# Output projection as 2x2 blocks with seven products for each two row tiles

## The chip, the core and the metric

The kernel runs on one core of one Trainium2 chip. The metric is the device time of one execution in microseconds (us). Five engines run their own instruction streams: TensorE (PE in the rows, with its weight loads as PEld), VectorE (DVE), ScalarE (ACT), GpSimd (POOL), and SyncE (SP), which here issues nearly all DMAs. They meet only through semaphores.

## The reference

One layer over 1024 tokens of width 1024, all in float32. Two branches (an attention `y_a` and a gated mixing branch `y_b`, each 512 wide) are projected up, gated and added; the sum goes through one output projection, is added to the input and normalised:

```python
p_a = jnp.einsum('bse,ed->bsd', y_a, w_up_a[l])
p_b = jnp.einsum('bse,ed->bsd', y_b, w_up_b[l])
merged = jax.nn.sigmoid(g_a) * p_a + jax.nn.sigmoid(g_b) * p_b
x = x + jnp.einsum('bsd,de->bse', merged, w_out[l])
...
return rmsnorm(x, final_norm_g)
```

## The kernel before

A float32 product is made of three matmuls on float32r operands: every operand is split into a high part (a cast on ACT, `copy`, L157) and a low part (the difference, `tt`, L167), and high x high, high x low and low x high are summed in PSUM. `hi_lo` (L214) issues the cast and the difference; the difference is on DVE unless the call names POOL.

The input projection already works by blocks: `project` (L528) takes two output tiles against two halves of the contraction and makes their four results by 7 products instead of 8, with the combinations of the small operand made on the fly (`s1` to `s4`) and those of the large one (`T`) once. Attention heads, projections and branch work are interleaved.

What this document looks at are the three last stages:

- `up_b` (L899) projects branch b up: 8 column tiles `e` by 2 halves of 512 tokens, 12 matmuls each; results go to DRAM (`merged_b`).
- `up_a` (L946) does the same for branch a, first half 0, then half 1. For each unit `up` (L882) loads the gate, runs 12 matmuls of 512 columns, multiplies PSUM by the gate on DVE; `merge` (L939) loads branch b's tile, adds it on DVE, and splits the sum into `m_hi` and `m_lo` (one cast, one more DVE operation). The 8 weights of `w_up_a` are split once (`wa`, L936) and serve both halves.
- The output projection: `out_unit` (L976) runs 24 matmuls of 512 columns (8 contraction tiles by 3) for one tile of 128 tokens and one half of the columns, with a slice of `m_hi` or `m_lo` as the stationary operand and `w_out`, split by `wo_parts` (L922), as the moving one. There are 16 such units; the last is cut into two of 256 columns. Behind each unit DVE adds `x`, ACT squares and sums; behind the second column half come the sum, the reciprocal root on POOL, and the two scaled halves go out.

The order of each engine is fixed when the program is built. `Plan.add` records every operation; `issue` (L234) plays them with a cost of its own for each and lets each engine take, of what is ready, the operation with the smallest number; a number can be moved ahead with `pl.offset` (`ahead`, L813, does this by 6000), except for PE. Every engine then runs its list strictly in that order, so that an operation that waits holds up all behind it. Buffers have tags with a fixed number of slots ("a" 7, "b" 8, "f2" 6, "T" 14, and the PSUM banks X, Y, Z, o once, z twice); a load is issued by SP, in SP's order, when a slot is free.

Of the kernel before, what the change touches and what calls it, by code (L numbers as in the profile page):

```python
# [329 lines left out]
def hybrid_block(  # L330
# [197 lines left out]
    def project(g, use, keep=True):  # L528

        use_at, pl.offset = pl.offset, -9000  # L530

# [5 lines left out]
        raw = {}  # L537
        for q in ((0, 0), (1, 0), (1, 1), (0, 1)):
            raw[q] = buf("a", (P, 4, P))
            pl.load(raw[q].all, w_pairs[g, 2 * q[0] + q[1]].rearrange("p (k e) -> p k e", e=P))  # L540
# [22 lines left out]
        pl.tt(s2.all, s1.all, raw[0, 0].all, ALU.subtract)  # L563
# [9 lines left out]
        pl.tt(s3.all, raw[0, 0].all, raw[1, 0].all, ALU.subtract, eng="POOL")  # L573
# [335 lines left out]
    m_hi, m_lo = [], []  # L909
    for e in range(8):  # L910
        if e < 6:
            mt = buf("T", (P, 2, S), F32R)
            m_hi.append(mt[:, 0, :])
            m_lo.append(mt[:, 1, :])
        else:
            m_hi.append(buf("k", (P, S), F32R).all)
            m_lo.append(buf("k", (P, S), F32R).all)

    wo = [[], []]
    wo_tags = ["r"] * 4 + ["e"] * 4 + ["ak"] * 2 + ["f1"] * 2  # L920

    def wo_parts(kt, c):  # L922
        raw = buf("a")
        pl.load(raw.all, w_out[kt, :, c * 512:c * 512 + 512])
        if c == 0:
            if kt < 6:
                hi, lo = [buf(tag, dt=F32R).all for tag in wo_tags[2 * kt:2 * kt + 2]]
            else:
                t = buf("k", (P, 2, 512), F32R)
                hi, lo = t[:, 0, :], t[:, 1, :]  # L930
        else:
            hi, lo = wo1[kt // 4][0][:, kt % 4, :], wo1[kt // 4][1][:, kt % 4, :]
        pl.hi_lo(hi, lo, raw.all)
        wo[c].append((hi, lo))
# [115 lines left out]
```

## Time and profile before

| | us |
|---|---|
| median of 3 runs | 766.98 (766.76 to 767.42) |
| the profiled execution | 766.53 |
| its span in the trace | 764.7 |
| PE busy in the span | 735.0 (96%) |
| DVE busy | 575.0 (75%) |
| ACT busy | 433.5 (57%) |
| POOL busy | 308.8 (40%) |

The span is what the trace shows; 1.8 us of the execution lie outside it. PE is busy nearly all the time, so the end of the kernel is set by how much PE has to do and by the places where it waits. A busy share says little about the other engines: what matters is whether PE waits for them at one place.

### The profile page before, as it was taken

What the parts mean: (1) busy time and instruction counts of PE and PEld (TensorE: products, weight loads), DVE (VectorE), ACT (ScalarE), POOL (GpSimd) and SP (SyncE); (2) the same over time, 40 slices, a digit from 0 to 9 for tenths busy, and PEclk for the clock granted to TensorE, in tenths of its full rate; (3) what the DMA queues carried; (4) which work ended last, traced back from release to release, by engine and by line L of the source; (5) the groups of instructions that cost most, each with busy time, mean ns of one, the idle gap of its engine ahead of it and who ended that gap; (6) DMA issues with size and microseconds to landing.
All of it is one profiled execution on the core that took longest, in us unless ns stands there. A gap on an engine that the chain in (4) does not pass through costs nothing.

```text
span 764.7 us, 10791 instructions
## 1 busy us (share of the span) xinstructions
PE 735.0 (96%) x3524; PEld 606.4 (79%) x3524; DVE 575.0 (75%) x788; ACT 433.5 (57%) x920; POOL 308.8 (40%) x298
## 2 busy tenths in 40 slices
PE   4989999999889999999999999999999999999996
PEld 3877788888777888887888888878888887888885
DVE  4868754688899787898999988897998878841122
ACT  6636474756756755666757676676867433411122
POOL 1500637497666576274345538234140300013110
PEclk9999999999999999999999999999999999999999
DMA  9412494424344375454543656354597677760022
GB/s 338 176 64 96 144 255 159 146 96 138 113 127 127 103 212 185 141 166 137 153 124 114 191 165 180 108 137 127 173 311 255 213 237 231 252 228 1 29 82 111
DMA packets 69177, 121.31 MB, mean 159 GB/s; under 512 B 7296, under 2 KB 17024, under 8 KB 69120
## 3 DMA queue, kind: packets, MB, share of 16 engines
q1 hardware_dynamic: 67968, 118.52, 49.3%
q10 hardware_dynamic: 1152, 2.10, 0.7%
q8 instruction: 28, 0.46, 0.3%
q14 instruction: 29, 0.24, 0.1%
HBM read 81.27 MB, written 39.32 MB: 158 GB/s over the span
## 4 chain that ended last, share of the span: by engine, by line
PE 83%; DVE 9%; issue 3%; DMA 2%; ACT 2%; POOL 1%; SPq 0%; POOLq 0%; DVEq 0%; ACTq 0%
PE Y L129 22%; PE X L129 21%; PE Z L129 18%; PE z L129 9%; PE o L129 8%; PE tr L133 5%; DVE b L167 2%; DVE ak L198 1%; DVE ak L191 1%; DMA k<-in_x_dram 1%; DVE e L167 1%; DMA k<-d 1%; DVE T L167 1%; DVE f L167 1%; DVE r L167 1%
## 5 line engine op out<-in xcount | busy, mean ns | idle before, releaser
L129 PE MATMUL Y<-T,b 128*128 128x512 f32 x672 | 180.0, 398 | 1.6 <-ACT b L157 1.3
L129 PE MATMUL X<-T,b 128*128 128x512 f32 x660 | 177.9, 398 | 0.0
L129 PE MATMUL Z<-T,b 128*128 128x512 f32 x540 | 145.2, 397 | 0.0
L129 PEld LDWEIGHTS Y<-T,b 128*128 128x128 f32 x672 | 122.3, 188 | 26.0 <-ACT b L157 1.7
L157 ACT CAST b<-a 128x512 fp32r<-128x512 f32 (+1 forms) x152 | 93.6, 617 | 81.9 <-PE Y L129 22.5
L129 PEld LDWEIGHTS X<-T,b 128*128 128x128 f32 x660 | 119.8, 188 | 22.8 <-POOL b L167 0.4
L167 DVE TENSOR_TENSOR b<-a,b 128x512 fp32r<-128x512 f32 (+1 forms) x112 | 99.4, 889 | 28.8 <-ACT b L157 20.0
L129 PEld LDWEIGHTS Z<-T,b 128*128 128x128 f32 x540 | 98.1, 188 | 18.3
L167 POOL TENSOR_TENSOR b<-a,b 128x512 fp32r<-128x512 f32 x40 | 60.7, 1516 | 119.8 <-ACT b L157 106.6
L198 DVE TENSOR_TENSOR_SCAN ak<-ak,c 128x128 f32<-128x128 f32 (+1 forms) x64 | 72.8, 1141 | 3.5 <-ACT ak L146 3.4
L167 POOL TENSOR_TENSOR a<-a,a 128x512 f32<-128x512 f32 x40 | 61.5, 1537 | 28.9 <-DVE b L167 15.3
L167 POOL TENSOR_TENSOR f<-f,f 128x512 f32<-128x512 f32 (+1 forms) x38 | 56.2, 1484 | 36.0 <-ACT f L146 14.7
L157 ACT CAST e<-tr 128x512 fp32r<-128x512 f32 (+1 forms) x96 | 45.7, 480 | 36.5 <-PE tr L133 33.3
L167 POOL TENSOR_TENSOR r<-r,ak 128x512 f32<-128x512 f32 x32 | 46.9, 1474 | 39.4 <-DVE ak L191 33.4
L133 PE MATMUL tr<-c,r 128*128 128x128 f32 x320 | 58.5, 273 | 2.6 <-DVE r L167 2.5
L129 PE MATMUL o<-e,k 128*128 128x512 f32 (+1 forms) x192 | 57.6, 343 | 3.3 <-DVE e L167 3.2
L146 ACT ACTIVATE ak<-z 128x128 f32<-128x128 f32 (+2 forms) x96 | 47.4, 494 | 20.4 <-PE z L129 18.1
L129 PE MATMUL z<-k,k 128*128 128x512 f32 (+2 forms) x216 | 56.8, 352 | 0.9 <-DMA k<-d 0.9
L167 DVE TENSOR_TENSOR e<-tr,e 128x512 fp32r<-128x512 f32 (+1 forms) x96 | 52.0, 545 | 7.3 <-ACT e L157 6.4
L146 ACT ACTIVATE r<-z 128x128 f32<-128x128 f32 (+2 forms) x96 | 46.9, 495 | 13.1 <-PE tr L133 12.5
L133 PEld LDWEIGHTS tr<-c,r 128*128 128x128 f32 x320 | 39.9, 140 | 13.6 <-DVE r L167 3.4
L191 DVE TENSOR_TENSOR_SCAN ak<-ak,c 128x512 f32<-128x512 f32 x32 | 50.5, 1588 | 0.2
(217 smaller groups left out, 1148.5 us busy)
## 6 DMA issues: line engine op xcount, KB each, us to landing
d<-f SPq DMA_DIRECT2D x112, 256.0 KB, 2.8
a<-in_w_pairs_dram SPq DMA_DIRECT2D x80, 256.0 KB, 2.8
f<-d SPq DMA_DIRECT2D x72, 256.0 KB, 3.2
k<-d SPq DMA_DIRECT2D x48, 256.0 KB, 4.8
k<-in_x_dram SPq DMA_DIRECT2D x8, 512.0 KB, 7.2
d<-b SPq DMA_DIRECT2D x16, 256.0 KB, 2.3
k<-d SPq DMA_DIRECT2D x8, 512.0 KB, 6.3
a<-in_w_up_dram SPq DMA_DIRECT2D x16, 256.0 KB, 4.3
```

The source lines that it names most:

```text
L129: lambda: self.nc.tensor.matmul(out.ap(), lhsT=lhsT.ap(), rhs=rhs.ap(), start=start, stop=stop, **kw),
L133: self.add("PE", 0.109, lambda: self.nc.tensor.transpose(out=out.ap(), in_=in_.ap(), identity=ident.ap()), [out], [in_, ident])
L146: return self.nc.scalar.activation(out=out.ap(), in_=in_.ap(), func=func, scale=sc, **kw)
L157: lambda: self.nc.scalar.copy(out=out.ap(), in_=in_.ap()), [out], [in_])
L167: self.add(eng, cost, lambda: e.tensor_tensor(out=out.ap(), in0=in0.ap(), in1=in1.ap(), op=op), [out], [in0, in1])
L191: lambda: self.nc.vector.tensor_tensor_scan(out.ap(), in_.ap(), in_.ap(), 1.0 if init is None else init.ap(), op0=ALU.mult, op1=ALU.bypass),
L198: lambda: self.nc.vector.tensor_tensor_scan(out.ap(), in_.ap(), floor.ap(), init, op0=ALU.mult, op1=ALU.max), [out], [in_, floor])
```

## The change

The output projection uses the scheme of the input projection. `project` is cut in two: `project` loads the four raw weight tiles and hands them to a new function `seven`, which holds the seven products and the sums behind them. `out_pair` calls `seven` for each two row tiles of 128 tokens: `raw` is then the merged activations (two row tiles by two halves of the contraction), and the moving operand `T` is `WT`, the seven combinations of the four quarters of `w_out`, each split in high and low parts. So 4 pairs of row tiles take 7 products of 12 matmuls with 512 columns.

Where the operands come from changes too:

- `merge` keeps the merged sum in float32 (`m0` for half 0, `m1` for half 1, the latter in two additions of 256 columns) and no longer splits it. `seven` makes the combinations and splits for each pair: 7 casts, 5 low parts on DVE and 2 on POOL, 2 combinations on POOL and 2 on DVE.
- `WT[1]`, `WT[5]` and `WT[6]` are made ahead of the first half of `up_a` (`w_out_first`), the other four during its second half (`w_out_rest(kt)` for a quarter `kt` after units 3, 5, 6 and 7). The first makes 12 loads, 12 casts, 12 POOL and 8 DVE operations of 512 columns; the second makes 16 loads, 16 casts, 16 POOL and 12 DVE operations. Before, `w_out` took 16 loads, 16 casts and 16 DVE operations.
- The weights of `w_up_a` are loaded and split for each half anew, into "b" slots: 16 loads, casts and low parts instead of 8.
- The last unit is no longer cut in two.

```diff
     def project(g, use, keep=True):
...
+        raw = {}
+        for q in ((0, 0), (1, 0), (1, 1), (0, 1)):
+            raw[q] = buf("a", (P, 4, P))
+            pl.load(raw[q].all, w_pairs[g, 2 * q[0] + q[1]].rearrange("p (k e) -> p k e", e=P))
+            raw[q] = raw[q].all
+        pl.offset = use_at
+        seven(raw, T, use, keep)
+
+    def seven(raw, T, use, keep):
...
+    WT = {}
+
+    def w_out_quads(kt, qs):
+        raw = {}
+        for kh, c in qs:
+            raw[kh, c] = buf("a")
+            pl.load(raw[kh, c].all, w_out[4 * kh + kt, :, c * 512:c * 512 + 512])
+        return raw
+
+    def w_out_split(i, kt, v):
+        hi, lo = [t[kt].all if isinstance(t, list) else t[:, kt, :] for t in WT[i]]
+        pl.hi_lo(hi, lo, v.all, "POOL" if i < 3 else "DVE")
+
+    def w_out_first():
+        for i in (1, 5, 6):
+            WT[i] = pair_of()
+        for kt in range(4):
+            q = w_out_quads(kt, ((0, 0), (0, 1), (1, 1)))
+            w_out_split(1, kt, q[0, 0])
+            pl.tt(q[0, 1].all, q[0, 1].all, q[0, 0].all, ALU.subtract, eng="POOL")
+            w_out_split(5, kt, q[0, 1])
+            pl.tt(q[1, 1].all, q[1, 1].all, q[0, 1].all, ALU.subtract, eng="POOL")
+            w_out_split(6, kt, q[1, 1])
...
+    def w_out_rest(kt):
+        q = w_out_quads(kt, ((1, 0), (1, 1), (0, 1), (0, 0)))
+        w_out_split(2, kt, q[1, 0])
+        pl.tt(q[0, 1].all, q[1, 1].all, q[0, 1].all, ALU.subtract, eng="POOL")
+        w_out_split(7, kt, q[0, 1])
+        w_out_split(3, kt, q[1, 1])
+        pl.tt(q[0, 0].all, q[0, 0].all, q[0, 1].all, ALU.add, eng="POOL")
+        pl.tt(q[0, 0].all, q[1, 0].all, q[0, 0].all, ALU.subtract, eng="POOL")
+        w_out_split(4, kt, q[0, 0])
...
+        if half == 0:
+            pl.tt(m0[kh][:, kt, :], t.all, t1.all, ALU.add)
         else:
...
+            for n in range(2):
+                cs = slice(256 * n, 256 * n + 256)
+                pl.tt(m1[kh, 2 + n][:, kt, :], t[:, cs], t1[:, cs], ALU.add)
...
-            up(0, e, half, wa[e], tags, merge)
...
+            w = up_weights(0, e, buf("b", (P, 512), F32R).all, buf("b", (P, 512), F32R).all)
+            up(0, e, half, w, tags, merge)
+            between(e)
...
+    load_y(0, 0)
+    ahead(w_out_first)
     ahead(up_a, 0, "XYZ")
-    up_a(1, TAGS)
...
+    load_y(0, 1)
+    ahead(up_a, 1, "XYZ", lambda e: w_out_rest({3: 0, 5: 1, 6: 2, 7: 3}[e]) if e in (3, 5, 6, 7) else None)
...
+        def use(j, c, v, in_psum):
+            res[j, c] = buf("a")
+            rs = res[j, c].all
+            pl.load(rs, x[rows[j], half_of(c)])
+            pl.tt(rs, v, rs, ALU.add)
+            ss[j, c] = small()
+            junk = buf("f2")
+            pl.act(junk.all, rs, AF.Square, scale=1.0 / 32, accum=ss[j, c])
+            if c == j:
+                pl.tt(rs, rs, fg[c].all, ALU.mult, eng="POOL")
+            else:
+                pl.stt(ss[j, c], ss[j, c], EPS, ss[j, 1 - c], ALU.add, ALU.add)
+                r = small()
+                pl.rsqrt(r, ss[j, c], nhalf[:, 0:1])
+                finish(j, 1 - c, r)
+                finish(j, c, r)
+        seven(mq, WT, use, False)
+
+    for g in range(4):
+        out_pair(g)
```

How the lists change is shown at three places. The first is POOL in the second half of `up_a`. Before, its list there (`os` is attention's last product with its gate, `r` attention's weights, `c` and `T` belong to the ends of the output units) reads:

```order
L167 TENSOR_TENSOR r_6551<-r_6551,ak_6508 128x512
L167 TENSOR_TENSOR r_6630<-r_6630,ak_6568 128x512
L167 TENSOR_TENSOR os_6367<-os_6367,f_4771 128x512
L181 TENSOR_SCALAR c_7266<-c_7266 128x1
L167 TENSOR_TENSOR T_7234<-T_7234,b_6576 128x512
```

and now (`a` are quarters of `w_out` and their combinations, T_7041 the low part of `WT[2]`, T_6830 and T_6963 the merged sums of half 0, b_7380 a low part for product 2 of the first pair):

```order
L167 TENSOR_TENSOR os_6345<-os_6345,f_4771 128x512
L167 TENSOR_TENSOR T_7041<-a_6996,T_7025 128x512
L167 TENSOR_TENSOR a_7028<-a_7020,a_7028 128x512
L167 TENSOR_TENSOR a_7054<-a_7054,a_7028 128x512
L167 TENSOR_TENSOR a_7054<-a_6996,a_7054 128x512
...
L167 TENSOR_TENSOR T_7041<-a_7247,T_7025 128x512
L167 TENSOR_TENSOR a_7298<-T_6830,T_6963 128x512
L167 TENSOR_TENSOR T_6830<-T_6830 128x4x128
L167 TENSOR_TENSOR a_7268<-a_7257,a_7268 128x512
L167 TENSOR_TENSOR a_7276<-a_7276,a_7268 128x512
L167 TENSOR_TENSOR a_7276<-a_7247,a_7276 128x512
L167 TENSOR_TENSOR a_7369<-T_6830,T_6963 128x512
L167 TENSOR_TENSOR b_7380<-T_6963,b_7361 128x512
```

Between attention's last product and the low part for product 2 of the first pair there are now 19 POOL operations of 512 columns (8 of them left out above), where there were none.

The second place is DVE behind the last unit of the first half of `up_a`. Before (k_6988 and k_7012 are high parts of the merged sum, T_7014 the low part of the second half of `y_a`, k_7027 and T_7064 low parts of `w_out`):

```order
L167 TENSOR_TENSOR k_7008<-f_6930,k_6988 128x512
L167 TENSOR_TENSOR T_7014<-a_6496,T_6980 128x512
L167 TENSOR_TENSOR T_7014<-a_6519,T_6980 128x512
L167 TENSOR_TENSOR k_7025<-f_6954,k_7012 128x512
L167 TENSOR_TENSOR T_7014<-a_6543,T_6980 128x512
L167 TENSOR_TENSOR T_7014<-os_6367,T_6980 128x512
L167 TENSOR_TENSOR k_7027<-a_6822,k_7027 128x512
```

Now (T_7009 is the low part of the second half of `y_a`, b_7058 of a weight of `w_up_a`, f_7066 of `WT[3]`, T_7088 of `WT[7]`, k_7115 and k_7120 the merged sum of half 1):

```order
L167 TENSOR_TENSOR f_6981<-X_7001,f_6981 128x512
L167 TENSOR_TENSOR T_6963<-f_6981,f_6988 128x512
L167 TENSOR_TENSOR b_7058<-a_6959,b_7036 128x512
L167 TENSOR_TENSOR f_7066<-a_7020,ak_7052 128x512
L167 TENSOR_TENSOR T_7009<-a_6747,T_6965 128x512
L167 TENSOR_TENSOR T_7009<-a_6807,T_6965 128x512
L167 TENSOR_TENSOR T_7009<-os_6345,T_6965 128x512
L167 TENSOR_TENSOR T_7088<-a_7028,T_7073 128x512
L167 TENSOR_TENSOR f_7005<-Y_7030,f_7005 128x512
L167 TENSOR_TENSOR k_7115<-f_7005,f_7014 128x256
L167 TENSOR_TENSOR k_7120<-f_7005,f_7014 128x256
```

From the multiply that empties the last unit of the first half (X_7001) up to the combination `s2` of the first pair, DVE has 47 operations now: 9 that read a PSUM bank, 22 of 512 columns with both operands in SBUF, and 16 of 256 columns with both in SBUF.

The third place is the end of DVE's list. Before (T_7297 is the last result tile, c_7266 the sums of squares):

```order
L167 TENSOR_TENSOR T_7297<-X_7697,T_7297 128x256
...
L167 TENSOR_TENSOR c_7266<-c_7266,s_7752 128x1
L167 TENSOR_TENSOR T_7297<-Y_7730,T_7297 128x256
L167 TENSOR_TENSOR c_7266<-c_7266,s_7767 128x1
L173 SCALAR_TENSOR_TENSOR T_7297<-T_7297,s_7772,b_6584 128x512
```

Now (a_7892 and a_7912 are the two result tiles that DVE finishes, X_7813 holds the last product):

```order
L167 TENSOR_TENSOR a_7912<-X_7813,a_7912 128x512
L173 SCALAR_TENSOR_TENSOR s_7962<-s_7962,s_7924 128x1
L173 SCALAR_TENSOR_TENSOR a_7892<-a_7892,s_7967,os_7096 128x512
L173 SCALAR_TENSOR_TENSOR s_7969<-s_7969,s_7945 128x1
L173 SCALAR_TENSOR_TENSOR a_7912<-a_7912,s_7976,os_6787 128x512
```

Behind the last product DVE has five operations where it had three, and the first of them is of 512 columns instead of 256.

## Rows read from the trace of the kernel before

**Rows 1.** Windows: length; busy us of PE, PEld, DVE, ACT, POOL; clock, DMA, GB/s.
```profile
200.00:260.00 60.00, 55.09 (x266) 44.14 (x266) 54.74 (x64) 39.86 (x87) 37.35 (x30) 1.00 0.38 114
560.00:600.00 40.00, 40.00 (x201) 33.32 (x200) 34.46 (x53) 25.12 (x59) 5.70 (x10) 1.00 0.81 277
625.00:647.50 22.50, 22.50 (x101) 18.61 (x100) 17.71 (x28) 8.43 (x15) 1.80 (x1) 1.00 0.76 239
647.50:670.00 22.50, 21.15 (x93) 17.19 (x92) 20.03 (x32) 10.42 (x19) 0.00 (x0) 1.00 0.75 244
```

**Rows 2.** Chain that ended last, in order: start, us, engine and line, matmuls merged.
```profile
665.43 2.72 PE Y L129 x12
...
670.87 10.91 PE z L129 x48
...
752.58 2.89 PE X L129 x24
```

**Rows 3.** Timeline of PE: start, us, operation, count, and the wait before it.
```profile
650.16 0.96 PE L129 MATMUL Y<-T,T 128*128 128x512 f32 x3 [1.35 <-DVE T L167]
```

**Rows 4.** Timeline of DVE and POOL at two places where both work.
```profile
157.56 3.00 POOL L167 TENSOR_TENSOR a<-a,a 128x512 f32<-128x512 f32 x2
157.81 1.59 DVE L167 TENSOR_TENSOR b<-a,b 128x512 fp32r<-128x512 f32 x1 [0.70 <-ACT b L157]
159.33 1.78 DVE L167 TENSOR_TENSOR r<-r,s 128x512 f32<-128x512 f32 x1
160.52 1.74 POOL L167 TENSOR_TENSOR r<-r,f 128x512 f32<-128x512 f32 x1
...
630.62 0.69 DVE L167 TENSOR_TENSOR ak<-a,ak 128x512 fp32r<-128x512 f32 x1
630.66 1.80 POOL L167 TENSOR_TENSOR os<-os,f 128x512 f32<-128x512 f32 x1 [16.70 <-DVE os L167]
631.34 0.69 DVE L167 TENSOR_TENSOR f<-X,f 128x512 f32<-128x512 f32 x1
631.95 1.06 DVE L167 TENSOR_TENSOR T<-f,T 128x512 fp32r<-128x512 f32 x1
```

**Rows 5.** Groups by line and form: busy, mean ns, idle before; and timeline rows of DVE.
```profile
L167 POOL TENSOR_TENSOR T<-T,b 128x512 f32<-128x512 f32 x8 | 10.3, 1291 | 0.6
L167 DVE TENSOR_TENSOR f<-X,f 128x512 f32<-128x512 f32 x8 | 5.5, 692 | 4.5 <-PE X L129 4.3
L167 DVE TENSOR_TENSOR T<-a,T 128x512 fp32r<-128x512 f32 x12 | 7.8, 683 | 0.4 <-ACT T L157 0.4
L157 ACT CAST T<-a 128x512 fp32r<-128x512 f32 x11 | 6.5, 620 | 3.9 <-DMA a<-in_w_out_dram 3.9
...
576.19 1.89 DVE L167 TENSOR_TENSOR T<-a,T 128x512 fp32r<-128x512 f32 x3
...
591.34 0.42 DVE L167 TENSOR_TENSOR r<-r,ak 128x256 f32<-128x256 f32 x1
```

**Rows 6.** The page: GB/s in 40 slices; DMA issues of 560 to 671: KB, us to landing.
```profile
GB/s 338 176 64 96 144 255 159 146 96 138 113 127 127 103 212 185 141 166 137 153 124 114 191 165 180 108 137 127 173 311 255 213 237 231 252 228 1 29 82 111
...
a<-in_w_out_dram SPq DMA_DIRECT2D x16, 256.0 KB, 4.3
```

**Rows 7.** Timeline of the end, and one full tile's addition at 747.
```profile
747.17 0.69 DVE L167 TENSOR_TENSOR T<-z,T 128x512 f32<-128x512 f32 x1 [2.38 <-PE z L129]
...
757.45 0.88 PE L129 MATMUL Y<-T,k 128*128 128x256 f32 x6
758.36 0.42 DVE L167 TENSOR_TENSOR T<-Y,T 128x256 f32<-128x256 f32 x1 [0.90 <-PE Y L129]
759.36 0.16 DVE L167 TENSOR_TENSOR c<-c,s 128x1 f32<-128x1 f32 x1 [0.58 <-ACT f L146]
759.60 0.55 POOL L167 TENSOR_TENSOR s<-c,c 128x1 f32<-128x1 f32 x1 [3.00 <-DVE c L167]
760.19 0.75 DVE L173 SCALAR_TENSOR_TENSOR T<-T,s,b 128x512 f32<-128x512 f32 x1 [0.66 <-POOL s L167]
```

More of the change, by code (lines that the diff above doesn't have):

```diff
@@ L535, in after @@
             pl.offset = -9000
[L537 to L540, printed above, removed]
         def parts(v, eng="DVE"):
             hi, lo = buf("b", (P, 4, P), F32R), buf("b", (P, 4, P), F32R)
-            pl.hi_lo(hi.all, lo.all, v.all, eng)
+            pl.hi_lo(hi.all, lo.all, v, eng)
             return hi, lo
@@ L550, in product @@
                 for a, b in ((w[0], T[i][0]), (w[0], T[i][1]), (w[1], T[i][0])):
-                    pl.mm(acc.all, a[:, kt, :], b[:, kt, :], start and n == 0, stop and n == 11,
-                          skip_group_check=True)
+                    pl.mm(acc.all, a[:, kt, :], b[kt].all if isinstance(b, list) else b[:, kt, :],
+                          start and n == 0, stop and n == 11, skip_group_check=True)
                     n += 1
@@ L572, in project @@
         s3 = raw[1, 0]
-        pl.tt(s3.all, raw[0, 0].all, raw[1, 0].all, ALU.subtract, eng="POOL")
+        pl.tt(s3, raw[0, 0], raw[1, 0], ALU.subtract, eng="POOL")
         product(2, w2, xx, False)
@@ L907, in hybrid_block @@
     ahead(up_b)
[L909 to L914, printed above, removed]
-        else:
[L916 to L934, printed above, removed]
@@ L936, in hybrid_block @@
-    wa = [buf("T", QUAD, F32R) for _ in range(4)]
-    wa = [up_weights(0, e, wa[e // 2][:, 2 * (e % 2), :], wa[e // 2][:, 2 * (e % 2) + 1, :]) for e in range(8)]
-    def merge(e, half, t):
-        fs = half_of(half)
-        t1 = buf("f2")
-        pl.load(t1.all, merged_b[e][:, fs])
-        pl.tt(t.all, t.all, t1.all, ALU.add)
-        pl.hi_lo(sub(m_hi[e], fs), sub(m_lo[e], fs), t.all)
-    def up_a(half, tags):
-        load_y(0, half)
-        for e in range(8):
-            up(0, e, half, wa[e], tags, merge)
@@ new lines, in w_out_first @@
+    def w_out_first():
[8 more added lines that the diff above has]
+            w_out_split(6, kt, q[1, 1])
+    for i in (2, 7):
+        WT[i] = pair_of()
@@ new lines, in hybrid_block @@
+    WT[3] = [[buf(tag, dt=F32R) for _ in range(4)] for tag in ("ak", "f1")]
+    WT[4] = [[buf(tag, dt=F32R) for _ in range(4)] for tag in ("r", "e")]
+    def w_out_rest(kt):
[7 more added lines that the diff above has]
+        w_out_split(4, kt, q[0, 0])
@@ new lines, in hybrid_block, with merge @@
+    m0 = [buf("T", QUAD) for _ in range(2)]
+    m1 = {(kh, pair): buf("k", (P, 4, 256)) for pair in (2, 3) for kh in range(2)}
+    def merge(e, half, t):
+        kh, kt = e // 4, e % 4
+        t1 = buf("f2")
+        pl.load(t1.all, merged_b[e][:, half_of(half)])
+        if half == 0:
+            pl.tt(m0[kh][:, kt, :], t.all, t1.all, ALU.add)
+        else:
+            for n in range(2):
+                cs = slice(256 * n, 256 * n + 256)
+                pl.tt(m1[kh, 2 + n][:, kt, :], t[:, cs], t1[:, cs], ALU.add)
```

78 lines of the change are left out of this document (23 added, 55 removed).

## Prediction

> **What bounds the kernel now.** I read the windows first [rows 1]. From 560 to 647.5 PE is busy all the time (40.00 of 40, 22.50 of 22.5), at a granted clock of 1.00, which is its higher level of 2.4 GHz; in the second half of `up_a` (647.5 to 670) it is busy 21.15 of 22.50. Then the chain of waits [rows 2]: from 670.87 it is PE matmuls end to end up to the last one, which ends at 757.45 + 0.88 = 758.33 [rows 7]. So the end is set by PE's work and by its waits; the only wait of weight in the last 150 us is one of 1.35 us for DVE [rows 3]. The windows show a second thing: in the second half of `up_a` DVE is busy 20.03 of 22.50 while POOL is busy 0.00 [rows 1]. This is the stretch into which the change puts most of its new work, and on those two engines.
>
> **The change part by part.**
>
> *Matmuls.* Before, 15 units of 24 matmuls of 512 columns and 48 of 256 run from 670.87 to 758.33: 87.46 us. After, 4 pairs take 4 x 7 x 12 = 336 of 512 columns. Twelve take 2.72 us [rows 2], 0.2267 each, so 76.2 us: **11.3 less**, all of it on the path. The units of `up_a` and `up_b` keep their number. The Trainium skill ("TensorE: Matmul & The Clock Gate", section "Back-to-back issue gap") gives about 131 ns as the sustained time of a matmul with 512 columns; by it the 48 matmuls less would be worth 6.3 us, an estimate from that page. The row's 227 ns is what this kernel pays.
>
> *The stretch behind the first half of `up_a`.* Let A be the end of that half's last unit. From A until product 2 of the first pair may run on, PE has 8 units of 12, products 1, 5 and 6, and one matmul ahead: 133 x 0.2267 = 30.2 us. In the same time DVE must get from the multiply of that last unit to `s2` of the pair, 47 operations. Alone they cost: 31 full ones at 0.60 (0.68 to 0.69 each, but three in a row take 1.89 [rows 5], so 0.09 overlaps), 9 of them with a PSUM operand and 22 with both in SBUF, and 16 of 256 columns, both in SBUF, at 0.33 (0.42 [rows 5] less that overlap): 5.4 + 13.2 + 5.3 = 23.9 us, which fits. POOL must get through 19 operations of 512 columns; the first can be over by A, the other 18 need loads that get their slots only about then. At 1.29 alone [rows 5] these are 23.2 us, which fits too.
>
> They do not fit together if DVE and POOL exclude each other, and rows show that they do. At 157.56 POOL starts two additions; DVE's difference of two SBUF operands, from 157.81, ends at 159.40: 0.55 behind 158.85, where POOL's first is over if it took its 1.29. POOL's second ends at 160.56, so two took 3.00 instead of 2.58; DVE's next took 1.78, POOL's next 1.74 [rows 4]. At 630.66 a POOL operation that starts just behind a DVE one takes 1.80; DVE's multiply out of PSUM at 631.34 takes its 0.69 beside it; the next DVE operation on two SBUF operands takes 1.06 and ends 0.55 behind POOL's [rows 4]. So the two take turns, and only DVE's operations with a PSUM operand run beside POOL's. The sum is then 23.2 + 13.2 + 5.3 = 41.7 us, and 0.6 for the first multiply, and behind `s2` two casts on ACT at 0.62 [rows 5] and POOL's low part for product 2 (1.29): 44.8 us against 30.2. **PE waits 14.6 us more.** The waits fall in several places: at the low parts of the second half of `y_a`, which now stand behind two other differences on DVE, at the low parts of `w_up_a`'s weights, which stand behind the additions of the unit before, and at products 5, 6 and 2 of the first pair. The bounds: if a turn costs POOL only the 0.42 that the 3.00 shows (18 turns with full operations at 0.42, the other 4 at 0.60), 11.4; if the engines also lose time to late loads (POOL idles where its operands land 4.3 us [rows 6] behind a slot that DVE frees late), some 5 more than 14.6, 20.
>
> The Trainium skill ("SBUF — State Buffer", section "Who interferes with whom") says that a DVE instruction with two SBUF inputs and a GpSimd instruction that reads SBUF block each other for the whole instruction. By it every turn would cost the whole 0.69 or 0.42: 23.2 + 15.2 + 6.7 and the 3.1 around them, 48.2 us, a wait of 18; the rows' 0.42 to 0.60 a turn say that some of an instruction lies outside.
>
> The wait of 1.35 before [rows 3] is at the same place and is part of the new one: **-1.35**.
>
> *Before A.* `w_out_first` brings 12 POOL operations, 15.5 us, into a time in which POOL is busy 5.70 of 40 and DVE 34.46 of 40 [rows 1]. Its 8 low parts on DVE stand where the 8 of `wa` stood, and the 8 of the first half's weights where `w_out`'s first and those of the merged sums stood, so DVE's count there is the same; what is new is that 12 POOL operations take turns with it. DVE has 5.5 us free in these 40, and about a third of its work reads PSUM. PE has `up_b` units to run meanwhile, but it is bound to its list. I take **+2**, with 0 and 5 as bounds (5: two thirds of 15.5 hold DVE, 10.3, less the free 5.5).
>
> *Pairs 2 to 4.* Per pair PE has 84 x 0.2267 = 19.0 us. DVE and POOL need: 9 full DVE operations on two SBUF operands and two scalings by 0.75 [rows 7], 6 POOL operations and two roots of 0.55 [rows 7]: 5.4 + 1.5 + 7.7 + 1.1 = 15.7, even without any overlap; ACT 16 operations at 0.62, 9.9. PE covers them: 0. With the cover gone the price would be what is over 19.0.
>
> *Transfers.* 12 more loads of `w_out` and 8 more of `w_up_a`, all ahead of the first pair. Where they decide is a rival, below.
>
> *The end.* Before, behind the last matmul (758.33): addition 0.42, square, sum, root 0.55, scaling from 760.19, over at 760.94: 2.61 us [rows 7]. Now the addition has 512 columns (0.69 [rows 7]), and DVE's list puts the other row tile's sum, its wait for a root and its scaling ahead of the last sum: 0.05 + 0.69 + 0.15, root 0.55 and 0.1 to get there and back, scaling 0.75, sum 0.15, root and way 0.65, scaling 0.75: 3.9. **+1.3.**
>
> *Sum:* -11.3 + 14.6 - 1.35 + 2 + 1.3 = +5.3. On the profiled execution's 766.53 that is 771.8; the median of the runs, 766.98, lies 0.45 above it, so 772.3. The case's own range: from -11.3 + 11.4 - 1.35 + 0 + 1.3 = 0 (767) to -11.3 + 20 - 1.35 + 5 + 1.3 = +13.7 (781).
>
> **The rivals.**
>
> *Faster: POOL's work slips in beside DVE's.* From 200 to 260 DVE is busy 54.74 and POOL 37.35 of 60 us and PE still gets 55.09 [rows 1]: both are full, and PE loses only 4.9. If POOL's operations fall where DVE waits for PE or reads PSUM, PE waits only for the order of DVE's list, 2 to 6 us, take 4: -11.3 + 4 - 1.35 + 1 + 1.3 = -6.3, 760.7. It decides if the turns cost DVE less than the 6.3 us that its 23.9 leave in 30.2, or 0.35 for each of 18 POOL operations. Against it: in those 60 us POOL has 30 operations, here 18 in half the time, and DVE's list has hardly a row that waits for nothing but PE.
>
> *About the same: transfers set the stretch.* From the first weight of the second half to the last quarter of `w_out`, SP's list has 46 transfers of 256 KB, 12.1 MB. The busiest slice moves 338 GB/s [rows 6], so these take 35.7 us; they can start some 4 us ahead of A, when the units before the last free their slots, so the last quarter is there at A + 31.7, and 7 POOL operations follow up to product 2's low part, 9.0: A + 40.7 against 30.2, a wait of 10.5, if turns cost little: -11.3 + 10.5 - 1.35 + 2 + 1.3 = +1.2, 768.1. For it: from 560 to 600 the DMA engines are busy 0.81 [rows 1]. Against it: SP issues a load when a slot is free, and DVE frees the slots, so that DVE comes first.
>
> *It does not do what it says:* fewer matmuls at another price. The first products' form, a stationary slice of 128 columns and a moving operand of 512, is the same as in the blocks of [rows 2], so I give this no chance of its own.
>
> **How the numbers follow.** The chances: the forecast (turns decide) 0.62, of which 0.06 falls within 0.2% of the time before; transfers 0.12, of which 0.08 within; POOL beside DVE 0.26, of which 0.22 faster and 0.04 within. What a measurement of this kernel can tell from no change is about 0.2%, 1.5 us. So faster 0.22, same 0.18, slower 0.60. The predicted time is the forecast's, 772.3, its own range 767 to 781. The range for 8 in 10 goes down to 761, which leaves out half of the faster case (0.12), and up to 780, which leaves out the forecast's end (0.06).
>
> **What would show it.** Right: POOL's operations in the second half of `up_a` take 1.7 to 1.8 us instead of 1.29, and DVE's on two SBUF operands over 1 us beside them; PE waits 10 to 20 us between A and product 2 of the first pair, mostly for DVE; 336 matmuls at 0.227 behind it; pairs 2 to 4 with no wait; some 3.9 us from the last matmul to the last scaling. Wrong: PE busy all through the first pair (then the rival of POOL beside DVE), or waits of ACT and POOL for loads of `w_out` while DVE idles (then transfers), or the waits ahead of A larger than those behind it.

## The result, and the profile after

| | us |
|---|---|
| median before (766.8 to 767.8) | 767.2 |
| median after (777.7 to 781.0) | 779.7 |
| ratio after to before, 95% interval | 1.016, 1.0134 to 1.0186 |
| forecast, with its range | 772.3, 761 to 780 |
| profiled execution after, its span | 780.95, 778.9 |

The change costs 12.5 us where the forecast had 5.3. Between the two traces (span +14.2) this divides at A, where the last unit of `up_a`'s first half ends; it is taken as the start of the first matmul behind that unit:

| | before | after | forecast |
|---|---|---|---|
| A | 647.28 | 650.65 | +2 (is +3.4) |
| A to the end of the last matmul | 111.04 | 120.69 | +1.95 (is +9.65) |
| last matmul to the end of the last scaling | 2.61 | 3.69 | +1.3 (is +1.1) |

The row of the kernel before that gives its A (its last matmul ends at 758.33 [rows 7]):

```profile
647.28 0.39 PE L129 MATMUL Y<-T,T 128*128 128x512 f32 x1
```

Behind A, PE now has 8 x 12 + 336 = 432 matmuls of 512 columns, at 0.2267 us 97.9 us. So it **loses 22.8 us** there; before it lost 2.2 (480 matmuls' worth, 108.8, in 111.04). "Lost behind A" is used in this sense below, for every kernel, from its profiled execution.

The windows of after, with the columns of [rows 1]: length; busy us of PE, PEld, DVE, ACT, POOL; granted clock, DMA share, GB/s.

```profile
653.50:706.00 52.50, 39.60 (x134) 29.80 (x134) 47.47 (x52) 16.54 (x30) 30.99 (x21) 0.84 0.57 184
...
694.00:701.00 7.00, 6.47 (x16) 4.71 (x16) 6.79 (x8) 2.84 (x6) 4.50 (x3) 0.52 0.23 77
724.00:771.00 47.00, 47.00 (x209) 38.80 (x207) 26.49 (x39) 21.71 (x46) 22.33 (x19) 1.00 0.30 100
```

The last row is the gain as forecast: in pairs 2 to 4 PE never waits, and matmuls follow each other at 0.2267. The first is where it goes: DVE is busy 47.47 of 52.50 and POOL 30.99, where before POOL had nothing [rows 1].

The timeline of PE in that stretch (start, us, operation, count, and the wait before it), with A at 650.65:

```profile
650.65 1.07 PE L129 MATMUL Y<-T,b 128*128 128x512 f32 x4
...
656.36 1.31 PE L129 MATMUL Y<-T,b 128*128 128x512 f32 x3 [2.83 <-DVE T L167]
...
669.98 4.14 PE L129 MATMUL Z<-T,b 128*128 128x512 f32 x10 [2.69 <-DVE b L167]
...
680.16 4.14 PE L129 MATMUL Y<-T,b 128*128 128x512 f32 x10 [3.07 <-DVE b L167]
...
693.85 0.78 PE L129 MATMUL Z<-T,b 128*128 128x512 f32 x2 [3.22 <-DVE f L167]
695.15 4.63 PE L129 MATMUL Z<-T,b 128*128 128x512 f32 x10 [0.53 <-DVE b L167]
...
703.30 2.66 PE L129 MATMUL X<-T,b 128*128 128x512 f32 x11
```

With one of 0.56 at 687.63 the waits are 12.9 us, all for DVE, where [rows 3] had one of 1.35. Taken alone the waits look like the forecast's 14.6, but PE also runs slowly: behind three of them the rows of ten matmuls are 4.1 to 4.6 us long instead of 2.4, at the lower clock level (0.52 in the window at 694). The 133 matmuls that the prediction counts take 52.65 us (650.65 to 703.30) instead of 30.2, and so nearly all of the 22.8 is lost there; behind 703.30 only 0.3 is. DVE and POOL in the same stretch:

```profile
678.36 1.75 DVE L167 TENSOR_TENSOR b<-a,b 128x512 fp32r<-128x512 f32 x1
680.03 1.77 DVE L167 TENSOR_TENSOR f<-a,ak 128x512 fp32r<-128x512 f32 x1
681.73 1.77 DVE L167 TENSOR_TENSOR b<-a,b 128x512 fp32r<-128x512 f32 x1
...
694.41 0.68 DVE L167 TENSOR_TENSOR b<-a,b 128x512 fp32r<-128x512 f32 x1
695.13 0.69 DVE L167 TENSOR_TENSOR a<-a,T 128x512 f32<-128x512 f32 x1
...
682.90 1.74 POOL L167 TENSOR_TENSOR T<-a,T 128x512 fp32r<-128x512 f32 x1
684.60 1.73 POOL L167 TENSOR_TENSOR a<-T,T 128x512 f32<-128x512 f32 x1
```

They take turns, as in [rows 4]: one operation of each in 1.69 us, where POOL alone takes 1.29 and DVE 0.68 [rows 5]. The row at 694.41 is the low part on which product 5 of the first pair waits until 695.15; the one at 695.13 is `s2`. From 650.85 to the end of `s2`, 45.0 us, DVE idles only 1.47, and that for PE. At the end of the list, beside [rows 7]:

```profile
770.95 0.39 PE L129 MATMUL X<-r,b 128*128 128x512 f32 x1
...
771.38 0.69 DVE L167 TENSOR_TENSOR a<-X,a 128x512 f32<-128x512 f32 x1 [1.23 <-PE X L129]
...
774.28 0.75 DVE L173 SCALAR_TENSOR_TENSOR a<-a,s,os 128x512 f32<-128x512 f32 x1 [0.66 <-POOL s L167]
```

### The profile page after: what moved, and what is told of

It reads as the page before. It is cut to its first block, busy times and chain, and to the rows that moved or that the text cites. A ratio compares the mean times of both kernels' runs of the same rounds, so it can differ in the third digit from the quotient of the medians.

```text
span 778.9 us, 10904 instructions
## 1 busy us (share of the span) xinstructions
PE 733.4 (94%) x3452; PEld 600.5 (77%) x3452; DVE 627.5 (81%) x826; ACT 456.1 (59%) x962; POOL 371.0 (48%) x334
## 4 chain that ended last, share of the span: by engine, by line
PE 71%; DVE 13%; DMA 7%; issue 4%; ACT 3%; POOL 1%; SPq 0%; POOLq 0%; DVEq 0%; ACTq 0%
PE Y L129 20%; PE X L129 20%; PE Z L129 18%; PE o L129 5%; PE tr L133 4%; DVE b L167 3%; PE z L129 3%; DVE f L167 2%; DMA f<-d 2%; DVE ak L198 2%; DVE e L167 1%; DMA a<-in_w_out_dram 1%; DVE T L167 1%; DMA d<-f 1%; DMA a<-d 1%
## 5 line engine op out<-in xcount | busy, mean ns | idle before, releaser
L129 PE MATMUL Y<-T,b 128*128 128x512 f32 x828 | 222.1, 402 | 8.0 <-DVE b L167 3.1
L129 PE MATMUL X<-T,b 128*128 128x512 f32 x816 | 215.9, 396 | 0.0
L129 PE MATMUL Z<-T,b 128*128 128x512 f32 x660 | 179.7, 404 | 6.4 <-DVE b L167 3.2
L129 PEld LDWEIGHTS Y<-T,b 128*128 128x128 f32 x828 | 153.3, 191 | 40.9 <-DVE b L167 4.6
L157 ACT CAST b<-a 128x512 fp32r<-128x512 f32 (+1 forms) x180 | 110.8, 617 | 118.6 <-PE Y L129 31.7
L129 PEld LDWEIGHTS X<-T,b 128*128 128x128 f32 x816 | 149.4, 188 | 29.0 <-POOL b L167 0.4
L167 DVE TENSOR_TENSOR b<-a,b 128x512 fp32r<-128x512 f32 (+1 forms) x140 | 123.2, 881 | 34.1 <-ACT b L157 28.4
L129 PEld LDWEIGHTS Z<-T,b 128*128 128x128 f32 x660 | 123.3, 192 | 31.8 <-DVE b L167 4.2
L167 POOL TENSOR_TENSOR a<-a,a 128x512 f32<-128x512 f32 x60 | 92.6, 1544 | 40.5 <-DVE b L167 20.1
L129 PE MATMUL z<-k,k 128*128 128x128 f32 (+2 forms) x192 | 50.8, 349 | 1.3 <-DMA k<-d 0.8
```

The lines of the kernel that those rows point to most:

```text
L129: lambda: self.nc.tensor.matmul(out.ap(), lhsT=lhsT.ap(), rhs=rhs.ap(), start=start, stop=stop, **kw),
L157: lambda: self.nc.scalar.copy(out=out.ap(), in_=in_.ap()), [out], [in_])
L167: self.add(eng, cost, lambda: e.tensor_tensor(out=out.ap(), in0=in0.ap(), in1=in1.ap(), op=op), [out], [in0, in1])
```

## The experiments

All are edits of the changed kernel. Medians stand against 767.0 (766.97 to 767.25 in the six groups of runs) for the kernel before; the ratio is to the kernel before, with its 95% interval. In this table fill and y_ahead do the whole computation; the other edits leave work out or put other values in its place.

| kernel | median us | ratio | A | lost behind A |
|---|---|---|---|---|
| changed | 779.7 | 1.0134 to 1.0186 | 650.65 | 22.8 |
| rest_cut | 768.5 | 1.0012 to 1.0045 | 649.64 | 9.4 |
| pool_set | 769.2 | 1.0011 to 1.0039 | 650.09 | 11.0 |
| fill | 777.7 | 1.0115 to 1.0166 | 650.27 | 18.7 |
| few_loads | 776.0 | 1.0092 to 1.0145 | 649.85 | 17.4 |
| few_none | 768.3 | 0.9999 to 1.0024 | 650.83 | 11.1 |
| first_cut | 776.9 | 1.0104 to 1.0170 | 648.38 | 19.8 |
| both_cut | 767.7 | 0.9988 to 1.0020 | 648.05 | 12.6 |
| y_ahead | 773.6 | 1.0061 to 1.0105 | 650.98 | 15.3 |
| y_both_cut | 766.0 | 0.9967 to 1.0005 | 650.71 | 9.6 |
| y_few_none | 764.6 | 0.9953 to 0.9976 | 647.38 | 8.5 |
| y_few_nolow | 758.5 | 0.9856 to 0.9916 | 648.91 | 3.1 |

A and "lost behind A" come from one execution, the median from 4 to 10, and the two need not fit: rest_cut's profiled execution (766.23) is the fastest of its ten, fill's (776.52) the fastest of four, the changed kernel's (780.95) the slowest of four. In the six kernels from "changed" to few_none no edit bears on the work ahead of A, and their A lies between 649.64 and 650.83.

### Is it the turns? rest_cut and pool_set

```diff
 # rest_cut, w_out_rest: 12 times; tt_cut is the same operation on columns 0:8, planned at its full cost
-        pl.tt(q[0, 1].all, q[1, 1].all, q[0, 1].all, ALU.subtract, eng="POOL")
+        pl.tt_cut(q[0, 1].all, q[1, 1].all, q[0, 1].all, ALU.subtract, eng="POOL")
...
 # pool_set, in the same 12 places, on the first operand's tile
+            for n in (512, 512):
+                self.tc.keep_in_program_order(e.memset(out.ap()[:, 0:n], 0.5))
+            return e.memset(out.ap()[:, 0:128], 0.5)
```

> The 12 POOL combinations of w_out_rest work on 8 of their 512 columns only (so WT[7] and WT[4] are wrong there), while every engine's list keeps its order, and all loads, casts and low parts stay. Theory (DVE and POOL take turns, and their sum sets the stretch): 12 x 1.29 = 15.5 us of POOL time go, so PE's waits from A to product 2 of the first pair fall from 12.9 to under 4 us, the granted clock of that stretch goes back to 1.00, and the time falls by 13 to 19 us, to 761 to 767. Rival (the loads of w_out set the stretch): the waits stay and move to rows that wait for a load; the time falls by 3 us at most, 777 or more. DVE's rows on two SBUF operands go back to about 0.7 us by the theory.

> Each of the 12 POOL combinations of w_out_rest is replaced by constants written over the same tile (two of 512 columns and one of 128, so that POOL is held about as long, 1.1 to 1.4 us, but reads nothing); the output is not the reference's, and DVE's and PE's lists keep their order. Theory (DVE waits because the two engines exclude each other while both read SBUF): DVE's rows beside these go back to 0.7 us and the time falls as far as in rest_cut, to 767 to 770. Rival 1 (POOL's own time sets the pace, and DVE waits for its results): the time stays at 776 to 780 with DVE idle in place of busy. Rival 2 (whatever POOL does on SBUF holds DVE): DVE's rows stay at 1.7 us and the time at 776 to 780.

Both came out on the side of the turns. rest_cut falls by 11.2 us, less than the 13 to 19 named (the 12 short operations still hold POOL 0.4 to 0.5 each, PE's waits fall to 5.8 and not under 4, and 9.4 us are lost all the same). pool_set is the sharper of the two: POOL is held as long as by the combinations. Timeline of pool_set, POOL and DVE over the same 4 us, and then at a place where POOL has an operation that reads SBUF again:

```profile
662.08 1.11 POOL L231 MEMSET a<- 128x512 f32 x2
663.25 0.21 POOL L232 MEMSET a<- 128x128 f32 x1
663.39 1.11 POOL L231 MEMSET a<- 128x512 f32 x2
664.57 0.21 POOL L232 MEMSET a<- 128x128 f32 x1
...
662.50 0.68 DVE L167 TENSOR_TENSOR e<-a,r 128x512 fp32r<-128x512 f32 x1
663.10 0.68 DVE L167 TENSOR_TENSOR b<-a,b 128x512 fp32r<-128x512 f32 x1
...
665.10 0.69 DVE L167 TENSOR_TENSOR b<-a,b 128x512 fp32r<-128x512 f32 x1
...
679.48 1.35 POOL L167 TENSOR_TENSOR T<-T 128x512 f32<-128x512 f32 x1
...
679.61 1.76 DVE L167 TENSOR_TENSOR e<-a,r 128x512 fp32r<-128x512 f32 x1
```

POOL works without a gap, 1.32 us for each combination's place, and DVE's operations on two SBUF operands take their 0.68 beside it; beside a difference on POOL in the same kernel DVE's takes 1.76. So DVE waits neither for POOL's results nor because POOL is busy, but because POOL's combinations, unlike the constants, read SBUF. The Trainium skill ("SBUF — State Buffer", section "Who interferes with whom") says that a DVE instruction with two SBUF inputs contends with a GpSimd instruction that reads SBUF, not with one that only writes it, and calls the port pair that they share an exclusive lock; the trace agrees, with the limit that a turn of both takes 1.69 us, not 1.29 + 0.69.

### Is it the clock? fill

```diff
 # Plan.issue: extra matmuls into a spare bank, at the five waits of PE
+                for _ in range(fill.get(n_pe, 0)):
+                    self.tc.keep_in_program_order(self.filler())
...
+    pl.filler = lambda: nc.tensor.matmul(fill_acc.all.ap(), lhsT=fill_w[:, 0, 0:P].ap(), rhs=fill_w[:, 0, :].ap(),
+                                         start=True, stop=True)
```

> Complete computation; PE's list gets 46 extra matmuls of 512 columns into a spare PSUM bank that nobody reads, on operands that are long ready, at the five places behind A where PE waits (10, 10, 12, 12 and 2; 0.227 us each, so no longer than the waits of 2.83, 2.69, 3.07, 3.22 and 0.53). Theory 1 (the slow matmuls behind the waits cost their 9.7 us by themselves): with PE kept at work the granted clock of the stretch is 1.00, matmuls behind the waits take 0.227 instead of 0.41, and the time falls by 7 to 10 us, to 770 to 773. Theory 2 (DVE and POOL set the pace, PE only arrives earlier and waits longer): the clock is 1.00 too, but only the last slow group, ahead of product 2 (10 matmuls in 4.63 us, 2.4 too many), is gained: 776 to 778.5.

Theory 2 (777.7). Timeline of fill at one of the places, the extra matmuls and the ten behind them:

```profile
666.14 2.43 PE L1034 MATMUL o<-T 128*128 128x512 f32 x10
668.66 2.56 PE L129 MATMUL Z<-T,b 128*128 128x512 f32 x10
```

The ten matmuls take 2.56 us instead of 4.14, the granted clock from 653.5 to 696 is 1.00, and the median falls by only 2.0 us: what PE does faster, it waits longer for DVE. The runs of the two kernels overlap (776.5 to 779.9 against 777.7 to 781.0), so the 2.0 is not sharp; between the two profiled executions lie 4.4, of which 2.5 in the 23 matmuls behind the last wait (5.64 us, 693.23 to 698.87, instead of 8.15) and 1.5 ahead of it, where that wait ends 42.96 behind A instead of 44.50. The matmuls behind the last wait count in full, since no wait follows them.

### Is it the loads? few_loads and few_none

```diff
 # few_loads, w_out_rest
-        q = w_out_quads(kt, ((1, 0), (1, 1), (0, 1), (0, 0)))
+        q = w_out_quads(kt, ((1, 0),))
+        q[0, 1], q[0, 0] = buf("a"), buf("a")        # filled on POOL from q[1, 0]
...
 # few_none: besides, no combination; all four are split from q[1, 0]
+        for i in (2, 7, 3, 4):
+            w_out_split(i, kt, q[1, 0])
```

> w_out_rest loads only one of its four quarters for each kt (4 loads instead of 16) and makes the others from it, so its output is not the reference's; the casts, the 12 combinations on POOL and all low parts keep their number. In rest_cut, where only the combinations' time was gone, PE still lost 9.3 us between A and its last matmul (107.2 us for 432 matmuls worth 97.9), with ACT idle for loads of w_out and w_up_a ahead of every wait; in the changed kernel it lost 22.8. Theory 1 (only turns count, the forecast's reading: the longer of two chains decides): without the 12 loads PE still loses about 15 of the 22.8 and the time is 771 to 774 only if loads added to the turns, else 777 or more. Theory 2 (turns and loads add up, because a slot is given back by the DVE or POOL operation that stands behind its load, and the next load waits for the slot): 8 to 10 us go, 769 to 772, and what PE still loses is near the forecast's 14.6.

> As few_loads, and the 12 combinations on POOL are left out too (all four operands are split from the one quarter, so the output is not the reference's). Theory 2 (turns 13.5 and loads 9.3 are all that PE loses behind A): PE loses 1 to 4 us there, and the time is 757 to 761, which is the changed kernel's 779.7 less 19 to 22. If something else is in the stretch (the order of DVE's list, the clock), 763 or more.

Neither theory: few_loads gains 3.7, where theory 2 had 8 to 10, and few_none (768.3) is no better than rest_cut (768.5), which has all the loads. The loads are not the second half of the loss; theory 2 fell. In few_none the operands of `w_out` come early, and DVE's list makes their low parts ahead of what PE needs.

### Ahead of A: first_cut and both_cut

```diff
 # w_out_first: 8 times (both_cut: and the 12 of w_out_rest)
-            pl.tt(q[0, 1].all, q[0, 1].all, q[0, 0].all, ALU.subtract, eng="POOL")
+            pl.tt_cut(q[0, 1].all, q[0, 1].all, q[0, 0].all, ALU.subtract, eng="POOL")
...
```

> The 8 POOL combinations of w_out_first work on 8 of their 512 columns only (WT[5] and WT[6] are wrong there); all lists keep their order. Theory (these turns cost the 3.2 us ahead of A): A comes 2 to 3 us earlier, near 648, and the time is 776 to 778. Rival (A is later for the order of the lists or the added loads): A stays at 650.6 and the time within 1 us of 779.7.

> The 12 combinations of w_out_rest and the 8 of w_out_first work on 8 of their 512 columns only (the output is not the reference's); all lists keep their order. From rest_cut (11.2 us less than the changed kernel) and first_cut (2.8 less): if the two add up, 765 to 766.5, so that even without the time of any combination the kernel gains 1 us of the 11.3 that the matmuls are worth. If w_out_first's cost is only passed on to the stretch behind A, 767 to 769.

The 8 combinations cost 2.3 us of A's 3.4 (A comes at 648.38, earlier than in all of those six kernels). Together with rest_cut the gain is only 0.7 more, as if the cost were passed on to the stretch behind A. In the profiled executions A is 1.6 us earlier and 3.2 more are lost behind it, but much of this is the choice of executions: rest_cut's lies 2.2 below its median, both_cut's 0.6 above. With hardly any of the combinations' time left the kernel is just as fast as the one before, although PE has 11 us less to do.

### The order of DVE's list, and its length: y_ahead, y_both_cut, y_few_none, y_few_nolow

```diff
 # y_ahead (and y_both_cut = both_cut + this, y_few_none = few_none + first_cut + this)
-    load_y(0, 1)
+    ahead(load_y, 0, 1)
 # y_few_nolow = y_few_none, and in w_out_rest only the casts (WT[i] = high part twice):
 # 12 low parts on DVE and 4 on POOL are left out
-            w_out_split(i, kt, q[1, 0])
+            t = WT[i][0]
+            pl.copy(t[kt].all if isinstance(t, list) else t[:, kt, :], q[1, 0].all)
```

> Complete computation; only the numbers of the loads and splits of the second half of y_a are moved ahead (as those of up_a are), so that its low parts stand ahead of w_out's in DVE's list. Theory (DVE's list from A to the low part for product 5 is the chain, whatever its order): the first wait (2.83 us at 656) falls under 1 and the later ones grow by as much; the time stays within 1.5 us of 779.7. Rival (each wait is a matter of its own place in the list): 776 to 777.

Both theories were wrong: it takes 6.2 us less. Three of the four low parts of `y_a` stood beside POOL's combinations; in y_ahead two of them come ahead of A and the third before POOL's next combination. DVE in the changed kernel, and then in y_ahead:

```profile
654.56 3.44 DVE L167 TENSOR_TENSOR T<-a,T 128x512 fp32r<-128x512 f32 x2
657.92 1.76 DVE L167 TENSOR_TENSOR T<-os,T 128x512 fp32r<-128x512 f32 x1
```

```profile
647.07 1.29 DVE L167 TENSOR_TENSOR T<-a,T 128x512 fp32r<-128x512 f32 x2
...
653.32 0.68 DVE L167 TENSOR_TENSOR T<-os,T 128x512 fp32r<-128x512 f32 x1
```

5.20 us become 1.97: 3.2 of the 6.2; the rest is open. Without the combinations (both_cut to y_both_cut) the same move is worth 1.7, which is within the spread of the two.

> both_cut (the 20 combinations of w_out on 8 of their 512 columns, so that the output is not the reference's) with the loads and splits of the second half of y_a moved ahead as in y_ahead. Theory 1 (the 9 us that are left behind A are DVE's order: low parts of w_out stand ahead of what PE waits for): both gains add, 761 to 763. Theory 2 (what is left is DVE's own work and loads, and y_ahead's 6 us were turns that the other order avoided): 766 or more.

> y_both_cut with, in addition, 12 of the 16 loads of w_out_rest left out (all four operands of a quarter are split from one loaded quarter, without the 12 short operations on POOL), so the output is not the reference's. Theory 1 (the loads are what is left: 46 transfers of 256 KB where PE has 30 us of work): PE loses under 3 us behind A and the time is 757 to 761. Theory 2 (DVE's own list, 47 operations and the turns with POOL's 7 others): 763 to 766.

> y_few_none without the low parts of w_out_rest (12 on DVE, 4 on POOL): the high part stands in for the low one in the matmuls, so the output is not the reference's; casts, loads and matmuls keep their number. Theory (DVE's list up to the low part for the last weight of up_a sets PE's pace: 26.2 us there against PE's 87 matmuls, 19.7): with 10 of these 12 operations ahead of that point, 6 us or more (with their turns) leave the chain, it fits beside PE's work, PE loses under 3 us behind A, and the time is 757 to 760. Rival (something else holds PE there): 763 or more.

y_both_cut (766.0) and y_few_none (764.6) both went theory 2's way: 12 loads and the 12 short operations on POOL less are worth 1.4 us together. y_few_nolow (758.5) lies in the theory's 757 to 760, with 3.1 us lost where under 3 was named. Windows of y_few_none and then of y_few_nolow, over the first 26.5 us behind A:

```profile
647.50:674.00 26.50, 20.98 (x89) 15.98 (x87) 26.15 (x41) 11.30 (x21) 8.66 (x7) 0.99 0.71 243
```

```profile
647.50:674.00 26.50, 25.28 (x112) 20.60 (x112) 23.59 (x37) 14.05 (x26) 7.12 (x5) 1.00 0.87 290
```

In the first DVE is busy 26.15 of 26.50 us, and PE waits for the low part of the last weight of `up_a`, which lets it go on at 673.88. PE's row there, and three of DVE's:

```profile
673.88 3.90 PE L129 MATMUL Z<-T,b 128*128 128x512 f32 x10 [1.44 <-DVE b L167]
...
661.45 1.78 DVE L167 TENSOR_TENSOR b<-a,b 128x512 fp32r<-128x512 f32 x1
663.15 1.78 DVE L167 TENSOR_TENSOR f<-a,ak 128x512 fp32r<-128x512 f32 x1
664.85 1.79 DVE L167 TENSOR_TENSOR e<-a,r 128x512 fp32r<-128x512 f32 x1
```

87 matmuls stand ahead of that one, 19.7 us of work against 26.2 of DVE. Of the 26.2 some 4.8 are still turns, with the operations that POOL keeps (low parts of `WT[2]`, combinations of the first pair): four of DVE's operations take 1.8 instead of 0.68, and one pair of 256 columns 1.14 instead of 0.76. DVE's own work is the other 21.4, still more than PE's 19.7. With 12 of DVE's operations and 4 of POOL's gone, PE is busy 25.28 of 26.50, loses 3.1 us behind A, and the kernel takes 758.5, 1.1% less than the one before (it leaves work out, so this is a bound and no version). So what is left when the combinations and their loads are taken away is DVE's list with the turns that remain in it; y_few_nolow takes some of both out and doesn't tell them apart.

### Can the combinations be had cheaper?

Complete versions, the first three with the combinations on another engine, the others with them made earlier and stored:

```diff
 # rest_dve: w_out_rest's 12 and WT[2]'s low parts; all_dve: w_out_first's 8 too; y_all_dve: and y_ahead
-        pl.tt(q[0, 1].all, q[1, 1].all, q[0, 1].all, ALU.subtract, eng="POOL")
+        pl.tt(q[0, 1].all, q[1, 1].all, q[0, 1].all, ALU.subtract, eng="DVE")
...
 # early, early2, mid_y, early_y47: c-a, b-a, d-b, (c-a)-(d-b), d-(b-a) for each quarter
+        for o, x0, x1, i in ((c, c, a, 0), (a, b, a, 5), (b, d, b, 7), (c, c, b, 4), (d, d, a, 6)):
+            pl.tt(o, x0, x1, ALU.subtract, eng="DVE")     # early2, mid_y: "POOL"
+            if i:
+                pl.store(wc[i][kt].all, o)                # loaded again where they are split
```

> Complete computation; w_out_rest's 12 combinations and the 4 low parts of WT[2] are on DVE instead of POOL (the lists are planned anew). Theory (turns): 16 x 1.29 us of POOL leave the sum and 16 x 0.60 on DVE come in, 11 us less, so PE waits 2 to 6 us in the stretch and the time is 766 to 772. Rival 1 (two engines really share the work, so that putting it on one makes DVE the bound): 47 + 16 operations are some 33 us on DVE against 30.2 on PE, and with 5 of latency the time is 775 or more. Rival 2 (loads): unchanged, 778 to 781.

> Complete computation; all 20 combinations of w_out (8 in w_out_first, 12 in w_out_rest) and the low parts of WT[2] are on DVE, so POOL has only the low parts of WT[1] and the pairs' own work; lists planned anew. Theory (a combination costs the shared time 1.29 us on POOL and 0.60 on DVE): behind A the chain of DVE is some 11 us shorter than in the changed kernel (44.5 to the low part for product 5), ahead of A DVE has 4.8 us more of its own and 8 turns less: 772 to 777. Rival (with 16 + 12 operations more, DVE is the bound by itself): 778 or more.

> Complete computation; all_dve with y_ahead's move. If the two gains (5.2 and 6.2 us) add: 768 to 769. If both take away the same turns: 773 to 775.

> Complete computation; the 16 combinations of w_out's quarters (and the 4 sums in between) are made on DVE near 60 to 130 us, where DVE and POOL have room, and stored (16 stores of 256 KB); late in the kernel the products' operands are only loaded and split, so POOL keeps the 8 low parts of WT[1] and WT[2] alone. Theory (turns): the stretch behind A loses 15.5 us of POOL time, and the time ahead of A loses 10.3: PE's waits behind A under 4 us, clock 1.00, A back at about 647.5 if the early work costs nothing: 758 to 764. Rival (loads set the stretch, 28 of 256 KB as before): 775 or more. If the early work is not hidden, up to 5 us more, seen as waits of PE between 60 and 140.

> Complete computation; as in the kernel early, w_out's combinations are made near 50 to 130 us and stored, but on POOL, with the smallest claim on it and with loads as soon as slots are free, so that DVE's list there stays as in the changed kernel; the late loads come in the order of the products that use them (WT[2], WT[7], then WT[3] and WT[4] behind the last unit), and the low parts of the second half of y_a stand ahead of w_out's in DVE's list. Early lost 8.4 us ahead of 213 us, by waits of PE for DVE at 89, 110 and 132. Theory: these 8 us come back, and the wait for loads in the stretch (4.06 for ACT in early) falls by half: 761 to 766. Rival (any early work costs as much, since POOL's turns now delay DVE): 770 or more.

> Complete computation; the 20 operations that make w_out's combinations (one more each quarter than before, for the shared sums) are on POOL between 240 and 400 us, one quarter behind each of four blocks of gates, and their 16 results are stored and loaded again; late in the kernel POOL has 8 low parts of w_out. The late operands come product by product (WT[2], WT[7], WT[3], WT[4] behind units 4 to 7), and y_ahead's move is in. If the early work is hidden and the stretch loses the turns: 762 to 767. If POOL's early work costs DVE turns there, up to 8 more, seen as waits of PE between 240 and 420.

> Complete computation; as early (combinations on DVE near 90 to 130 us, 8.4 us late ahead of 213), with the late operands product by product and y_ahead's move as in mid_y. If the move and the order of the loads gain behind A what y_ahead gained: 768 to 770, with A near 656 and under 6 us lost behind it. If loads are what is left behind A: 773 to 775.

rest_dve 777.4, all_dve 774.5, y_all_dve 775.1: rest_dve gains 2.3 of the 8 to 14 named (and its runs, 775.4 to 780.7, overlap the changed kernel's), so its rival 1 came true: on DVE the combinations join the list that is too long. all_dve lies in its range; with y_ahead's move it gains nothing more. early 773.8, early2 776.9, early_y47 772.3: 9 to 11 us are lost behind A instead of 22.8, and the early work sets A back by 4.8 to 9.5 us, for it is not hidden there. All three miss the theory's times: early2 went its rival's way, early and early_y47 ended between the two. A wait of PE in early, where the changed kernel has none:

```profile
132.16 4.58 PE L129 MATMUL Y<-T,b 128*128 128x512 f32 x12 [2.80 <-DVE f L167]
```

mid_y, at 770.9 (ratio 1.0037 to 1.0081), has the lowest median: A at 655.79, so the early work is not hidden there either, and 7.6 us lost behind it; this is within what its expectation allowed for early work that costs turns. No complete version that was run beats the kernel before.

## Why the prediction had the direction and not the size

**Matmuls, -11.3: right.** PE runs pairs 2 to 4 at 0.2267 us a matmul without a wait (window 724 to 771); the 131 ns of the Trainium skill ("TensorE: Matmul & The Clock Gate", section "Back-to-back issue gap") is not what a matmul of 512 columns takes in any row here.

**The end, +1.3: right** (+1.1). **Pairs 2 to 4 covered: right.** There DVE is busy 26.49 and POOL 22.33 of 47 us.

**Before A, +2: within its bounds** (+3.4). 2.3 of it are w_out_first's combinations (first_cut).

**The stretch, +14.6: the term that failed.** It measured 22.8, and 22.8 - 2.2 - 14.6 + 1.35 = 7.35 us is most of the 8.9 by which the two traces differ beyond the forecast (14.2 against 5.3). The mechanism was the one forecast: pool_set shows that DVE waits because POOL reads SBUF, and the 12 combinations are worth 10.5 to 11.2 us. What failed is the step that made a wait of it. It compared DVE's and POOL's sum with PE's work once, at the end, product 2 of the first pair: 44.8 against 133 matmuls, 30.2 us. PE is held earlier. The last wait ends at 695.15, for product 5's low part: DVE's list had come nearly to its end, but only 110 of the 133 matmuls stand ahead of it, 24.9 us; the other 23 could not fill a wait that lies in front of them. By the forecast's own durations the sum up to there is 41.7, so 16.8 instead of 14.6.

Next, the sum itself ran longer: 45.0 us to the end of `s2` where it had 42.3. The forecast let the nine operations out of PSUM lie beside POOL's for nothing and POOL never pause; but POOL idled 18.0 of the 45 us (14.7 for loads and casts, 3.3 for DVE), and 1.5 DVE waited for PE. (Pauses for late loads were in the forecast's upper bound, 20; the measured loss lies beyond that too.) Up to the last wait this makes 19.6 (A to 695.15 is 44.5, less 24.9). The rest is the clock, which the forecast didn't have: the 23 matmuls behind the last wait take 8.15 us instead of 5.2, 2.9 more. 19.6 + 2.9 is 22.5 of the 22.8. fill, whose profiled execution takes 43.0 to the same place and 5.6 behind it, bears this out within the spread of its runs.

The same step had also said that DVE's 23.9 us alone "fit" into 30.2. Compared place by place, that isn't safe either: in y_few_none DVE is at work without a pause until the last weight's low part, 26.2 us, of which 21.4 are its own work, against PE's 19.7; y_few_nolow, where 12 operations of DVE and 4 of POOL are gone, loses 3.1 instead of 8.5.

**A single turn was dearer in the forecast than it is.** A POOL and a DVE operation take 1.69 together, 1.29 + 0.40, the lower of the two values that the prediction had (0.42 and 0.60). That the total came out higher although each turn is cheaper shows that the missing part was not in the price of a turn.

**The rivals.** POOL beside DVE: refuted by the rows of 1.75 and by pool_set. Transfers: few_loads takes 12 of the 16 late loads of `w_out` away and gains 3.7 us, y_few_none 1.4 over y_both_cut, with 12 short operations of POOL gone as well; they are a part, not the cause.

Open: whether an earlier A is partly lost again behind it, as both_cut suggests (0.7 gained for an A that is 1.6 earlier, within the spread of its runs); 3 of y_ahead's 6 us; and what the second split of `w_up_a`'s weights costs in the stretch, which no run took out.

## What to carry to other kernels

Whether an engine's new work fits is not a question of its sum over a stretch: go through its list and compare, at every operation that PE waits for, what stands ahead of it there with what PE has to do ahead of the same point. Work moved from DVE to POOL isn't moved away while both read two SBUF operands; it is cheap only where DVE idles or reads PSUM. And fewer matmuls pay only if the operands that they need are made where another engine has room: here PE saved 11 us, and the engines that make the operands were the ones already full.

## What was unexpected of the hardware

POOL's constants written to SBUF (1.11 us for two of 512 columns) don't hold DVE at all, which works at 0.68 beside them, while POOL's operations that read SBUF make the same operation 1.75. And PE's waits of 2.7 to 3.2 us are followed by ten matmuls at the lower of the two clock levels (0.40 to 0.44 us each; granted clock 0.52 in the window at 694), yet this counts for less than it seems while another engine sets the pace: with the clock held at 1.00 the median falls by 2.0 us (the runs overlap), not the 5.6 that these three groups of ten add up to (3.98, 3.98 and 4.43 us, start to start, instead of 2.27 each).
